# Order of VectorE and ScalarE in the attention stage: pieces, rows, weights and read-outs cut into single-engine steps

## The chip, the cores and the metric

The kernel runs on one core of one Trainium2 chip. The metric is device time in microseconds (us) of one execution; the median of several runs counts. TensorE (PE) multiplies matrices and transposes, VectorE (DVE), ScalarE (ACT) and GpSimd (POOL) work on elements, SyncE's queue (SP) issues the transfers (DMAs). Each engine takes its instructions from a queue of its own, in the order in which they stand there, and waits where an operand isn't ready.

## The reference, cut to what matters

One layer of an encoder on x of 2048 tokens by 1024 columns, all in float32:

```python
h = rmsnorm(x, attn_norm_w)
q_a, k_a, v_a, q_b, k_b, v_b, g_b, g_c, x_c = split(h @ w_in)     # 4 heads, 8 heads, 256 channels
y_sb = stick_breaking_attention(q_a, k_a, v_a)                    # sigmoid(z) * prod(1 - sigmoid(z)) over nearer keys
y_ch = chunked_relpos_attention(rms(q_b), rms(k_b), v_b, rel_bias)  # softmax over a band of 576 keys
y_cv = g_b * causal_conv3(g_c * x_c)
x = x + group_rmsnorm(concat(y_sb, y_ch, y_cv)) @ w_out
x = x + swiglu(rmsnorm(x, ffn_norm_w), w_gate, w_up, w_down)      # d_ff = 2816
```

The kernel holds the tokens in reversed order.

## The kernel before

**Stages.** The tokens are worked on in two halves of two groups (512 tokens, four blocks of 128 each). The attention stage (`weave`) holds all projections from w_in, both attentions and the convolution for both halves, and the output projection of the first half. Then come, without a hand-written order, the feed-forward part of the first half (`ffn(0)`), the output projection of the second half and `ffn(1)`.

**Products.** Each float32 product is made of three float16 products with a high and a low part of each factor (`mm3`, L318 to L323). So every weight block is prepared: `load` fetches it (L181) and ScalarE sums its squares (L183), `split` forms a power of two from the sums through one small matmul into a bank `tp` (L206 or L208) and small VectorE instructions (L212 to L220), then ScalarE scales (L225) and rounds it to the high part (L226), GpSimd takes the difference as the low part (L227), and both are stored in DRAM (`wd`, L231) for the next half. `get` hands out one block, splits the next and loads the one after.

**Rows.** Rows of 128 tokens are fetched into tiles `xt` (six buffers, also for `yt` and `xf`), normed by `rms_rows` (a Square on ScalarE, L310, a chain of ten [128,1] instructions, L312 and L103 to L116, and one product, L314, on VectorE), and turned by `to_T` (TensorE L275 into a bank `sc`, ScalarE `hh` L277, VectorE `hl` L278). `Rows.ahead` does a pair of rows; `beside` deals its yields out between the matmuls of a projection, one for every four steps, and `need` runs it at once.

**Pieces.** A stick-breaking piece is up to four key blocks for one block of queries: scores (L608, L611) into a bank `sc`, two sigmoids on ScalarE (`be` L634, `re` L635), on VectorE a running product (L636) and a product (L638). A piece of the chunked attention has up to five blocks: VectorE adds the bias and takes the maximum (L670, L674), ScalarE the exponential (L676), VectorE the factor `f` (L679, L680). Then in both `transposed`: TensorE turns up to four blocks into a bank `tp` (L574; two banks for five blocks), ScalarE reads the bank as `wth` (L576), VectorE as `wtl` (L577). At last `weighted` multiplies with V into the bank `av`, and `put_y` reads it (ScalarE `yu` L599, GpSimd L600, a store on SP L601). PSUM has 2 banks `acc`, 3 `sc`, 2 `tp` and 1 `av`. `piece` and `chunk_tile` hand out three functions: `front`, `mid` (the transposes with their read-outs) and `back`.

**Order.** `weave` walks through the 112 pieces of the first half and the 176 of the second. `fill` is a generator of the projections, which yields an estimate of TensorE's time; `run` advances it up to a clock value, and `later` puts a function off to a clock value. `stage` traces for piece i the `mid` of piece i - 3, then the `back` of piece i - 5, then the `front` of piece i, each followed by a third of the projections that belong to this piece. Only TensorE's queue keeps this order (`manual_schedule` with `engines={PE}`); the queues of the other engines are ordered by the compiler, which estimates when each instruction can start. A read-out (`use`) follows the last matmul of its bank at once.

Of the kernel before, what the change touches and what calls it, by code (L numbers as in the profile page):

```python
# [9 lines left out]
F32 = mybir.dt.float32  # L10
# [30 lines left out]
def trunk(ctx: ExitStack, tc: tile.TileContext, x, anw, w_in, qnw, knw, biasx, conv_w, onw, w_out,  # L41
# [44 lines left out]

    def acc():
        return ps.tile([128, 512], F32, name="acc", tag="acc", bufs=2)

    def sc1():  # L90
        return ps.tile([128, 512], F32, name="sc", tag="sc", bufs=3)

    def tpb():
        return ps.tile([128, 512], F32, name="tp", tag="tp", bufs=2)
# [66 lines left out]
    class Weights:  # L161
# [3 lines left out]
        def __init__(self, plan):  # L165
            self.plan = plan
            self.raw, self.ready = {}, {}
            self.at = 0

        def load(self, n):  # L170
            if n >= len(self.plan) or n in self.raw or self.plan[n] in wd:
                return
            key = self.plan[n]
            shape, one, gain, srcs = block(key)
            ss = small(2, "ws", BF16)
            tiles = []
            for i, unit in enumerate(srcs):
# [4 lines left out]
                with nc.allow_low_precision(reason="a bound, to a factor of two"):  # L182
                    nc.scalar.activation(junk(), raw, AF.Square, accum_out=ss[:, i:i + 1])  # L183
                tiles.append(raw)
            self.raw[n] = ss, tiles

        def split(self, n):
            if n >= len(self.plan) or n in self.ready:
                return
            key = self.plan[n]  # L190
            shape, one, gain, srcs = block(key)
# [9 lines left out]
            ss, tiles = self.raw.pop(n)  # L201
            m = len(tiles)
            o = tpb()
# [5 lines left out]
            c = 1 if one else m  # L209
# [20 lines left out]
            for w, t in zip(made, wd[key]):  # L230
                nc.sync.dma_start(t, w)  # L231
            self.ready[n] = made

        def ahead(self):
            self.split(self.at)
            self.load(self.at + 1)
# [809 lines left out]
```

## Time and profile before

| what | value |
|---|---|
| median of 3 runs | 2725.04 us (2721.22 to 2729.78) |
| the profiled execution | 2726.58 us |
| its span, first to last instruction | 2724.7 us |
| mean granted clock of TensorE | 0.98 of full speed |
| busy: PE, DVE, ACT, POOL | 2539.0, 1467.3, 1079.9, 401.3 us |
| first stage (to about 1180 us): busy PE, DVE, ACT | 1026.4, 914.7, 754.1 us |

An engine's busy time is that in which it executes an instruction; the rest of the span it waits or has nothing to do. Busy time in the two stages differs, so it is read by stretches. The profiled execution's time beyond its span lies around the first and last instruction.

### The profile page before, as it was taken

The page shows a single profiled execution, that of the slowest core. Times are in us where ns is not written, and L with a number is a line of the kernel's source. Part 1 is how long each engine was busy: PE and PEld are TensorE (multiplying, and loading weights), DVE is VectorE, ACT ScalarE, POOL GpSimd, SP SyncE. Part 2 cuts the span into 40 slices and gives each one's busy share as a digit, 9 for nine tenths or more (in the row PEclk, how much of TensorE's full clock was granted, in tenths as well). Part 3 has the DMA queues.
Part 4 walks back from the last instruction along what each step waited for, and adds up shares of the span by engine and source line. Part 5 has one row for each costly group of instructions (what it writes and reads, how often), then busy time and mean ns, then how long its engine had stood idle before and what let it go on. Part 6 is the DMA issues. An engine that isn't in the chain of part 4 may idle for free.

```text
span 2724.7 us, 41834 instructions
## 1 busy us (share of the span) xinstructions
PE 2539.0 (93%) x16258; PEld 1690.5 (62%) x16258; DVE 1467.3 (54%) x3455; ACT 1079.9 (40%) x1994; POOL 401.3 (15%) x469
## 2 busy tenths in 40 slices
PE   5988888998799888979999999999999999999999
PEld 4567766766687577845555555556865555555556
DVE  6467877789989877844443334334342333223233
ACT  5566756666466777762333333320121111111110
POOL 2124331112313121121111121110000000000000
PEclk8999999999899999989999999999999999999999
DMA  7443435434221256372222223222651111111101
GB/s 246 142 128 97 124 112 159 129 123 146 92 81 47 97 167 194 94 271 102 93 93 93 93 99 110 93 101 98 226 194 39 47 47 49 68 47 47 47 24 62
DMA packets 245352, 294.34 MB, mean 108 GB/s; under 512 B 77472, under 2 KB 194208, under 8 KB 245152
## 3 DMA queue, kind: packets, MB, share of 16 engines
q1 hardware_dynamic: 245152, 291.65, 33.2%
q8 instruction: 128, 2.10, 0.3%
q14 instruction: 72, 0.59, 0.1%
HBM read 199.30 MB, written 92.27 MB: 107 GB/s over the span
## 4 chain that ended last, share of the span: by engine, by line
PE 37%; DMA 5%; issue 4%; DVE 2%; POOL 1%; ACT 1%; SPq 1%; POOLq 0%; DVEq 0%; ACTq 0%
PE acc L321 7%; PE acc L322 7%; PE acc L320 7%; PE sc L963 5%; PE sc L965 5%; PE sc L964 5%; DMA x1d<-xs 2%; DMA wr<-in_w_down 1%; POOL w L227 1%; DMA wr<-in_w_up 1%; PE sc L275 0%; DVE gl L949 0%; DVE wl L260 0%; DVE x L967 0%; ACT wh L258 0%
## 5 line engine op out<-in xcount | busy, mean ns | idle before, releaser
L321 PE MATMUL acc<-hl,w 128*128 128x512 f16 x1728 | 656.1, 380 | 0.2 <-DVE hl L278 0.2
L320 PE MATMUL acc<-hh,w 128*128 128x512 f16 x1728 | 656.2, 380 | 0.0
L322 PE MATMUL acc<-hh,w 128*128 128x512 f16 x1728 | 655.9, 380 | 0.0
L945 DVE SCALAR_TENSOR_TENSOR sg<-acc,ds,sg 128x512 f32<-128x512 f32 x88 | 66.0, 750 | 614.8 <-PE acc L322 539.5
L320 PE MATMUL acc<-w,hh 128*128 128x256 f16 x1408 | 391.6, 278 | 4.0 <-ACT w L226 4.0
L321 PE MATMUL acc<-w,hh 128*128 128x256 f16 x1408 | 391.6, 278 | 1.8 <-POOL w L227 1.8
L322 PE MATMUL acc<-w,hl 128*128 128x256 f16 x1408 | 391.3, 278 | 0.0
L967 DVE TENSOR_TENSOR x<-sc,x 128x512 f32<-128x512 f32 x352 | 241.4, 691 | 211.0 <-PE sc L965 203.6
L322 PEld LDWEIGHTS <-w 128*128 128x128 f16 x1728 | 169.3, 98 | 205.3 <-issue 2.2
L963 PE MATMUL sc<-wh,gh 128*128 128x512 f32 x704 | 282.3, 401 | 4.6 <-DVE x L967 4.5
L320 PEld LDWEIGHTS <-w 128*128 128x128 f16 x1728 | 169.4, 98 | 183.9 <-issue 5.6
L321 PEld LDWEIGHTS <-w 128*128 128x128 f16 x1728 | 169.3, 98 | 180.1 <-issue 0.6
L965 PE MATMUL sc<-wh,gl 128*128 128x512 f32 x704 | 278.0, 395 | 0.0
L964 PE MATMUL sc<-wl,gh 128*128 128x512 f32 x704 | 277.9, 395 | 0.0
L227 POOL TENSOR_TENSOR w<-wr,w 128x1024 f16<-128x1024 f32 x76 | 162.4, 2157 | 547.1 <-ACT w L226 463.9
L577 DVE SCALAR_TENSOR_TENSOR wtl<-tp,wth 128x512 f16<-128x512 f32 (+3 forms) x384 | 200.2, 530 | 46.9 <-ACT wth L576 45.9
L636 DVE TENSOR_TENSOR_SCAN re<-re,zero 128x512 f32<-128x512 f32 (+3 forms) x160 | 187.7, 1173 | 63.2 <-ACT re L635 63.0
L576 ACT ACTIVATE wth<-tp 128x512 f16<-128x512 f32 (+3 forms) x384 | 176.1, 475 | 81.2 <-PE tp L574 80.2
L948 ACT CAST gh<-sg 128x512 fp32r<-128x512 f32 x88 | 54.3, 617 | 384.4 <-DVE sg L945 384.4
L225 ACT ACTIVATE wr<-wr,wsc 128x1024 f32<-128x1024 f32 x76 | 83.4, 1142 | 194.5 <-DVE wsc L216 194.2
L321 PEld LDWEIGHTS <-hh 128*128 128x128 f16 x1408 | 140.5, 100 | 31.5 <-issue 5.7
L963 PEld LDWEIGHTS sc<-wh,gh 128*128 128x128 f32 x704 | 132.5, 188 | 41.3 <-DVE x L967 8.9
(167 smaller groups left out, 3776.2 us busy)
## 6 DMA issues: line engine op xcount, KB each, us to landing
w<-wd SPq DMA_DIRECT2D x92, 512.0 KB, 4.1
wd<-w SPq DMA_DIRECT2D x76, 512.0 KB, 2.7
wr<-in_w_down SPq DMA_DIRECT2D x44, 512.0 KB, 4.4
q<-qd SPq DMA_DIRECT2D x192, 64.0 KB, 2.3
wr<-in_w_gate SPq DMA_DIRECT2D x22, 512.0 KB, 4.4
wr<-in_w_up SPq DMA_DIRECT2D x22, 512.0 KB, 5.4
xt<-in_x SPq DMA_DIRECT2D x16, 512.0 KB, 4.7
wr<-in_w_in SPq DMA_DIRECT2D x16, 512.0 KB, 5.3
```

Source lines behind the costliest of these rows:

```text
L225: nc.scalar.activation(raw, raw, AF.Copy, scale=sc[:, 0:1] if one else sc[:, i:i + 1])
L227: nc.gpsimd.tensor_tensor(w[:, 1, :], raw, w[:, 0, :], ALU.subtract)
L320: nc.tensor.matmul(o, sh(k), mh(k), start=(k == 0), stop=False)
L321: nc.tensor.matmul(o, sh(k), ml(k), start=False, stop=False)
L322: nc.tensor.matmul(o, sl(k), mh(k), start=False, stop=(k == n - 1))
L576: nc.scalar.activation(wh[:, s], tp[:, c], AF.Copy, scale=WSC)
L577: nc.vector.scalar_tensor_tensor(wl[:, s], tp[:, c], WSC, wh[:, s], op0=ALU.mult, op1=ALU.subtract)
L636: nc.vector.tensor_tensor_scan(re, re, zero.to_broadcast([128, N]), 1.0 if b == T else e[:, 0:1], ALU.mult, ALU.add)
L963: nc.tensor.matmul(o, gh[:, cs], wh[:, cc], start=st, stop=False)
L964: nc.tensor.matmul(o, gh[:, cs], wl[:, cc], start=False, stop=False)
L965: nc.tensor.matmul(o, gl[:, cs], wh[:, cc], start=False, stop=en)
L967: nc.vector.tensor_tensor(x1, o, x1, ALU.add)
```

## The change

VectorE and ScalarE join TensorE: their queues keep the order in which the program is traced in the first stage. For that the program is cut into steps that hold the work of one engine where that was done:

- A piece is one generator (`steps`). A `beat` is a third of a `stage`; on each beat every piece in flight counts down and, at zero, is advanced by one step; a yield gives the number of beats to the next. TensorE's scores, then a beat later the next engine's step, and so on. Of the two sigmoids, `re` is now the first.
- PSUM banks carry a note (`Bank`) of whether their read-out has been traced. Who asks for a bank whose last holder's hasn't been has it traced then.
- Read-outs of projections are traced 0.8 us of the projections' clock later (`behind`), those of `to_T` after its yield.
- A weight block's Squares move from `load` to `split`; `split` is a generator, which `start` begins 2.0 us after a `get` and goes on with after 3.0 us and 1.5 us for each tile.
- Rows are fetched a pair ahead, and `rms_rows` norms a pair with [128,2] instructions (13 in the chain), in a step for ScalarE and one for VectorE, whose yields are 0.0. `y_norm`'s rows are fetched 5 us before their norm.
- After the first stage these steps are run through at once (`stream.paced = False`).

Repeated adaptions to the new return values are left out.

```diff
+        def read(self, what):
+
+            def once():
+                if not self.done:
+                    self.done = True
+                    what()
+            self.force = once
+            return once
+
...
+    def bank(name, bufs, cols=512):
+        ring = Bank.rings.setdefault(name, [])
+        if len(ring) == bufs:
+            old = ring.pop(0)
+            while not old.done:
+                old.force() if old.force is not None else advance(old.piece)
+        ring.append(Bank())
+        return ps.tile([128, cols], F32, name=name, tag=name, bufs=bufs), ring[-1]
...
-            for i, unit in enumerate(srcs):
+            for unit in srcs:
                 raw = wp.tile([128, D], F32, name="wr", tag="wr", bufs=4)
                 rv = raw.rearrange(f"p ({shape[0]}) -> p {shape[0]}", **shape[1])
                 for put, src in unit:
                     nc.sync.dma_start(put(rv), src)
-                with nc.allow_low_precision(reason="a bound, to a factor of two"):
-                    nc.scalar.activation(junk(), raw, AF.Square, accum_out=ss[:, i:i + 1])
                 tiles.append(raw)
-            self.raw[n] = ss, tiles
+            self.raw[n] = tiles
...
             self.load(n)
-            ss, tiles = self.raw.pop(n)
+            shape, one, gain, srcs = block(key)
+            tiles = self.raw.pop(n)
+            self.ready[n] = made = []
             m = len(tiles)
-            o = tpb()
+            c = 1 if one else m
+            ss = small(2, "ws", BF16)
+            for i, raw in enumerate(tiles):
+                with nc.allow_low_precision(reason="a bound, to a factor of two"):
+                    nc.scalar.activation(junk(), raw, AF.Square, accum_out=ss[:, i:i + 1])
+            yield 3.0
+            o, bk = tpb()
...
-            made = []
+            wd[key] = [dp.tile([128, 2, D], F16, name=f"wd{len(wd)}_{i}") for i in range(m)]
             for i, raw in enumerate(tiles):
+                yield 1.5
                 w = wp.tile([128, 2, D], F16, name="w16", tag="w16")
                 nc.scalar.activation(raw, raw, AF.Copy, scale=sc[:, 0:1] if one else sc[:, i:i + 1])
                 nc.scalar.copy(w[:, 0, :], raw)
                 nc.gpsimd.tensor_tensor(w[:, 1, :], raw, w[:, 0, :], ALU.subtract)
+                nc.sync.dma_start(wd[key][i], w)
                 made.append(w)
-            wd[key] = [dp.tile([128, 2, D], F16, name=f"wd{len(wd)}_{i}") for i in range(m)]
...
+        def start(self, n, after=0.0):
+            self.steps[n] = self.split(n)
+            if self.paced:
+                later(after, lambda: self.more(n))
+            else:
+                run_all(self.steps[n])
+
+        def more(self, n):
+            after = next(self.steps[n], None)
+            if after is not None:
...
-            self.split(n)
+            if n not in self.steps:
+                self.steps[n] = self.split(n)
+            run_all(self.steps[n])
             self.load(n + 1)
-            if n:
-                self.ahead()
-            else:
-                later(6.0, self.ahead)
+            self.start(n + 1, 2.0)
+            self.load(n + 2)
...
         for i in range(2):
-            p = sc1()
+            p, bk = sc1()
             ks = slice(4 * i, 4 * i + 4)
             for k in range(4):
                 c = (4 * i + k) * 128
                 nc.tensor.transpose(p[:, k * 128:(k + 1) * 128], xn[:, c:c + 128], ident)
-            pk = p.rearrange("p (k c) -> p k c", k=4)
-            nc.scalar.copy(hh[:, ks, cs], pk)
-            nc.vector.tensor_tensor(hl[:, ks, cs], pk, hh[:, ks, cs], ALU.subtract)
+
+            def parts(pk=p.rearrange("p (k c) -> p k c", k=4), ks=ks):
+                nc.scalar.copy(hh[:, ks, cs], pk)
+                nc.vector.tensor_tensor(hl[:, ks, cs], pk, hh[:, ks, cs], ALU.subtract)
+
+            parts = bk.read(parts)
             yield 0.45
+            parts()
...
+    def rms_rows(tiles, gain):
+
+        a = small(2, "sa")
+        for i, xt in enumerate(tiles):
+            nc.scalar.activation(junk(), xt, AF.Square, accum_out=a[:, i:i + 1])
+        yield 0.0
+        nc.vector.tensor_scalar(a, a, -0.5 / D, -0.5 * EPS, op0=ALU.mult, op1=ALU.add)
+        r = rsqrt(a, 2, "rr")
+        for i, xt in enumerate(tiles):
+            nc.vector.scalar_tensor_tensor(xt, xt, r[:, i:i + 1], gain, op0=ALU.mult, op1=ALU.mult)
+        yield 0.0
...
+                tiles = self.get(g, t)
+                if t == 0:
+                    self.get(g, 2)
+                if self.norm is not None:
+                    yield from self.norm(tiles)
+                for b, xt in zip((t, t + 1), tiles):
+                    yield from to_T(xt, *self.H[g], b)
+                del self.got[g, t]
...
+    def behind(what):
+        if stream.paced:
+            later(0.8, what)
+        else:
+            what()
...
-            use(g, o)
+            behind(bk.read(lambda g=g, o=o: use(g, o)))
...
+        parts = [(0, 3), (3, 5)] if n == 5 else [(0, n)]
+        tps = []
+        for b0, b1 in parts:
+            tps.append(tpb())
+            for b in range(b0, b1):
+                nc.tensor.transpose(tps[-1][0][:, (b - b0) * 128:(b - b0 + 1) * 128],
+                                    src[:, b * 128:(b + 1) * 128], ident)
+        yield
+        for (tp, bk), (b0, b1) in zip(tps, parts):
+            nc.scalar.activation(wh[:, b0 * 128:b1 * 128], tp[:, :(b1 - b0) * 128], AF.Copy, scale=WSC)
+        yield
+        for (tp, bk), (b0, b1) in zip(tps, parts):
+            bk.done = True
             s = slice(b0 * 128, b1 * 128)
-            c = slice(0, (b1 - b0) * 128)
-            for b in range(b0, b1):
-                nc.tensor.transpose(tp[:, (b - b0) * 128:(b - b0 + 1) * 128],
-                                    src[:, b * 128:(b + 1) * 128], ident)
-            nc.scalar.activation(wh[:, s], tp[:, c], AF.Copy, scale=WSC)
-            nc.vector.scalar_tensor_tensor(wl[:, s], tp[:, c], WSC, wh[:, s], op0=ALU.mult,
+            nc.vector.scalar_tensor_tensor(wl[:, s], tp[:, :(b1 - b0) * 128], WSC, wh[:, s], op0=ALU.mult,
...
     def put_y(T, head, av, f):
+        av, bk = av
+        yield
+        bk.done = True
         u = ap.tile([128, 2 * HD], F32, name="yu", tag="yu")
         nc.scalar.activation(u, av, AF.Copy, scale=f)
+        yield
         nc.gpsimd.tensor_tensor(u[:, :HD], u[:, :HD], u[:, HD:], ALU.add)
...
+            def steps():
+                z, bk = scores(Q, cols, K, (b - k0) * 128, N, b == T)
+                yield
+                bk.done = True
...
+                nc.scalar.activation(re, z, AF.Sigmoid, scale=ZS[head // 2][:, 1:2])
                 nc.scalar.activation(be[:, :N], z, AF.Sigmoid, scale=ZS[head // 2][:, 0:1])
-                nc.scalar.activation(re, z, AF.Sigmoid, scale=ZS[head // 2][:, 1:2])
+                yield
                 nc.vector.tensor_tensor_scan(re, re, zero.to_broadcast([128, N]),
                                              1.0 if b == T else e[:, 0:1], ALU.mult, ALU.add)
                 MUL.tensor_tensor(be[:, 0:N], be[:, 0:N], e[:, 0:N], ALU.mult)
-
-            def mid():
-                r["T"] = transposed(r["w"], n)
-
-            def back():
+                yield 5
+                w = yield from turned(be, n)
+                yield 5
                 if b == T:
                     state["av"] = open_av()
                 av = state["av"]
-                weighted(av, *r["T"], [V[:, b + i - k0] for i in range(n)], b == T, b + n == NB)
+                weighted(av[0], *w, [V[:, b + i - k0] for i in range(n)], b == T, b + n == NB)
                 if b + n == NB:
...
-            for i, (a, w) in enumerate(parts):
-                z = scores(Q, cols, K, c0 + a, w)
+            zs = [scores(Q, cols, K, c0 + a, w) for a, w in parts]
+            yield
+            for i, ((z, bk), (a, w)) in enumerate(zip(zs, parts)):
+                bk.done = True
...
+            yield
...
+            yield 2
             f = small(1, "f")
             nc.vector.reciprocal(f, tot)
             nc.vector.tensor_tensor(f, f, VS[head], ALU.mult)
-            r["s"], r["f"] = s, f
...
+            yield 3
+            w = yield from turned(s, n)
+            yield 5
             av = open_av()
...
-                later(6.0 * (4 * i + t), lambda T=g * 4 + t: y_norm(
-                    T, gain, lambda: ap.tile([128, 520], F32, name="ysq", tag="w2")))
+                def start(T=g * 4 + t):
+                    yt = y_fetch(T)
+                    later(5.0, lambda: y_norm(T, yt, gain, lambda: ap.tile([128, 520], F32, name="ysq", tag="w2")))
+
+                later(6.0 * (4 * i + t), start)
...
+        def beat(gap):
+
+            for p in list(line):
+                p[0] -= 1
+                if p[0] == 0:
+                    advance(p)
+            run(clock[0] + gap / 3)
+
+        def stage(p, half, gap):
+            beat(gap)
+            beat(gap)
+            line.append([1, p, half])
+            beat(gap)
+
...
+                    spent += BLK * p[1]
+                    stage(p[0], half, max(0.0, origin + at * step - spent - clock[0]))
+        while line:
+            beat(1.0)
         run(1e9)
+        stream.paced = False
...
-        with tc.manual_schedule(engines={mybir.EngineType.PE}):
+        with tc.manual_schedule(engines={mybir.EngineType.PE, mybir.EngineType.DVE, mybir.EngineType.Activation}):
```

## Rows read from the trace of the kernel before

**Rows 1.** The page's busy line, and the span in 40 slices, in tenths.
```profile
PE 2539.0 (93%) x16258; PEld 1690.5 (62%) x16258; DVE 1467.3 (54%) x3455; ACT 1079.9 (40%) x1994; POOL 401.3 (15%) x469
...
PE   5988888998799888979999999999999999999999
...
DVE  6467877789989877844443334334342333223233
```

**Rows 2.** Stretches: busy PE, PEld, DVE, ACT, POOL; granted clock, DMA share, GB/s.
```profile
0.00:60.00 60.00, 26.24 (x192) 22.67 (x193) 40.68 (x140) 35.65 (x57) 14.18 (x21) 0.86 0.76 249
60.00:320.00 260.00, 237.88 (x1924) 174.21 (x1922) 163.98 (x343) 162.83 (x305) 76.22 (x100) 0.97 0.42 130
320.00:360.00 40.00, 28.67 (x248) 23.54 (x249) 37.65 (x149) 26.04 (x56) 18.05 (x20) 0.83 0.29 89
360.00:580.00 220.00, 205.00 (x1683) 143.56 (x1681) 156.92 (x530) 137.18 (x321) 45.15 (x89) 0.99 0.50 146
580.00:760.00 180.00, 151.47 (x1338) 116.39 (x1337) 175.13 (x347) 103.58 (x193) 49.36 (x49) 0.96 0.33 105
760.00:1180.00 420.00, 377.18 (x3626) 306.46 (x3625) 340.35 (x961) 288.80 (x604) 93.97 (x143) 0.98 0.39 117
1180.00:1220.00 40.00, 26.72 (x117) 14.68 (x116) 22.15 (x65) 26.29 (x39) 9.02 (x4) 0.79 0.89 313
1220.00:2725.00 1505.00, 1485.80 (x7142) 889.02 (x7140) 530.41 (x925) 299.54 (x422) 95.39 (x44) 1.00 0.25 86
```

**Rows 3.** TensorE's waits, 60 to 1180 us: total, times, longest.
```profile
PE tp L574 <- DVE wtl L577: 41.0, 36, 4.2
...
PE tp L517 <- DVE wtl L577: 10.6, 7, 2.7
...
PE tp L517 <- DVE qrt L111: 6.5, 1, 6.5
```

**Rows 4.** Timeline at 228 to 236 us: ScalarE, TensorE.
```profile
228.18 2.19 ACT L225 ACTIVATE wr<-wr,wsc 128x1024 f32<-128x1024 f32 x2
230.26 1.99 ACT L226 CAST w<-wr 128x1024 f16<-128x1024 f32 x2
...
235.39 1.11 PE L574 MATMUL tp<-ident,be 128*128 128x128 f32 x4 [4.21 <-DVE wtl L577]
```

**Rows 5.** Timeline at 1052 to 1059 us: ScalarE, VectorE, TensorE.
```profile
1055.75 1.06 ACT L310 ACTIVATE junk<-xf 128x1024 bf16<-128x1024 f32 x1 [3.75 <-DMA xf<-x1d]
...
1056.93 0.15 DVE L312 TENSOR_SCALAR sa<-ss 128x1 f32<-128x1 f32 x1 [4.03 <-ACT junk L310]
...
1059.04 1.02 PE L574 MATMUL tp<-ident,s 128*128 128x128 f32 x5 [4.65 <-DVE f L679]
```

**Rows 6.** Groups by line and shape, 60 to 1180 us: busy, mean ns, idle before.
```profile
L496 POOL TENSOR_TENSOR qs<-qk 128x512 f32<-128x512 f32 x32 | 37.3, 1166 | 46.2 <-ACT qk L494 46.2
...
L183 ACT ACTIVATE junk<-wr 128x1024 bf16<-128x1024 f32 x28 | 29.8, 1064 | 23.0 <-DMA wr<-in_w_in 22.9
L500 DVE TENSOR_REDUCE qa<-qs 128x8 f32<-128x512 f32 x32 | 21.7, 677 | 11.7 <-POOL qs L496 9.6 <-POOL re L630 1.9
...
L314 DVE SCALAR_TENSOR_TENSOR xf<-xf,rry,gain 128x1024 f32<-128x1024 f32 x4 | 5.1, 1281 | 0.0
```

**Rows 7.** Timeline of the start: TensorE's wait, ScalarE ahead of it.
```profile
36.81 1.05 ACT L310 ACTIVATE junk<-xt 128x1024 bf16<-128x1024 f32 x1
...
45.55 1.94 PE L275 MATMUL sc<-ident,xt 128*128 128x128 f32 x8 [15.56 <-DVE xt L314]
```

**Rows 8.** Timeline of VectorE: a solid chain, then a woven one.
```profile
233.78 0.18 DVE L111 TENSOR_TENSOR qrt<-qrt,qa 128x16 f32<-128x16 f32 x1
233.99 0.17 DVE L113 SCALAR_TENSOR_TENSOR qry<-qrt,qry 128x16 f32<-128x16 f32 x1
...
694.84 0.17 DVE L111 TENSOR_TENSOR qrt<-qrt,qa 128x16 f32<-128x16 f32 x1
694.93 0.68 DVE L740 TENSOR_REDUCE ya<-ysq 128x8 f32<-128x512 f32 x1
```

More of the change, by code (lines that the diff above doesn't have):

```diff
@@ L85, in trunk, with __init__, advance @@
     ynd = [dp.tile([128, D], F32, name=f"ynd{t}") for t in range(NB)]
+    class Bank:
+        rings = {}
+        def __init__(self):
+            self.done = False
+            self.piece = running[0]
+            self.force = None
+        def read(self, what):
[5 more added lines that the diff above has]
+            return once
+    running = [None]
+    def bank(name, bufs, cols=512):
[6 more added lines that the diff above has]
+        return ps.tile([128, cols], F32, name=name, tag=name, bufs=bufs), ring[-1]
     def acc():
-        return ps.tile([128, 512], F32, name="acc", tag="acc", bufs=2)
+        return bank("acc", 2)
     def sc1():
-        return ps.tile([128, 512], F32, name="sc", tag="sc", bufs=3)
+        return bank("sc", 3)
     def tpb():
-        return ps.tile([128, 512], F32, name="tp", tag="tp", bufs=2)
+        return bank("tp", 2)
+    def advance(p):
+        before, running[0] = running[0], p
+        wait = next(p[1], "over")
+        running[0] = before
+        if wait == "over":
+            line.remove(p)
+            traced[p[2]] -= 1
+        else:
+            p[0] = wait or 1
+    line = []
+    traced = [None, None]
     def small(n, name, dt=F32):
@@ L227, in split @@
                 nc.gpsimd.tensor_tensor(w[:, 1, :], raw, w[:, 0, :], ALU.subtract)
+                nc.sync.dma_start(wd[key][i], w)
                 made.append(w)
-            wd[key] = [dp.tile([128, 2, D], F16, name=f"wd{len(wd)}_{i}") for i in range(m)]
[L230 to L236, printed above, removed]
+        def start(self, n, after=0.0):
[7 more added lines that the diff above has]
+            if after is not None:
+                later(after, lambda: self.more(n))
         def get(self, key):
@@ L391, in beside, with normed, norm, fetch @@
             yield from more
+    def normed(key):
+        gain = []
+        def norm(tiles):
+            if not gain:
+                gain.append(gain_row(key))
+            yield from rms_rows(tiles, gain[0])
+        return norm
     def x_rows(H, groups):
-        gain = []
-        def make(g, b):
+        def fetch(g, b):
             xt = xp.tile([128, D], F32, name="xt", tag="xt")
@@ L399, in make, with fetch @@
             nc.sync.dma_start(xt, x[r0:r0 + 128, :])
-            if not gain:
-                gain.append(gain_row("a"))
-            return rms_rows(xt, gain[0])
-        return Rows(H, groups, make)
+            return xt
+        return Rows(H, groups, fetch, normed("a"))
     def y_rows(H, groups):
-        def make(g, b):
+        def fetch(g, b):
             yt = xp.tile([128, D], F32, name="yt", tag="xt")
@@ L748, in y_norms @@
     def y_norms(half):
[L749 removed]
+        assert traced[half] == 0, (half, traced)
         groups = HALVES[half]
@@ L777, in ffn_rows, with fetch @@
     def ffn_rows(H, groups):
-        gain = []
-        def make(g, b):
+        def fetch(g, b):
             xt = xp.tile([128, D], F32, name="xf", tag="xt")
             last_row[where(g)[0]] = nc.sync.dma_start(xt, x1d[g * 4 + b])
-            if not gain:
-                gain.append(gain_row("f"))
-            return rms_rows(xt, gain[0])
-        return Rows(H, groups, make)
+            return xt
+        return Rows(H, groups, fetch, normed("f"))
     HF = [{}, {}]
@@ L871, in weave @@
         ends = [whole + start + 8.0, 2 * whole + 11.6 * unit / 1.4]
[L872 to L873 removed]
         BLK = 0.5
[L876 to L887 removed]
+        def beat(gap):
[9 more added lines that the diff above has]
+            beat(gap)
         for half, groups in enumerate(HALVES):
             pieces, blocks = count(half)
+            traced[half] = pieces
             origin = None
```

114 lines of the change are left out of this document (40 added, 74 removed).

## Prediction

> **What bounds the kernel now.** Read the page's first two parts before anything else [rows 1]. TensorE is busy 93% of the span, VectorE 54%, ScalarE 40%; but the slices fall into two stages. In the first 17 (1,160 us, the attention stage) VectorE stands mostly at 6 to 9 tenths and TensorE between 5 and 9; behind them, but for the slice of the change-over, TensorE is at 9. So the second stage is TensorE's, and whatever an order of VectorE and ScalarE is worth must come out of the first. The table of stretches gives the amount [rows 2]. TensorE stands idle 60 - 26.2 = 33.8 us up to 60 us, 22.1 us from 60 to 320, 11.3 from 320 to 360, 15.0 from 360 to 580, 28.5 from 580 to 760 and 42.8 from 760 to 1180: 119.7 us after the start. From 1220 on it is 19 us in 1,505.
>
> In two of these stretches VectorE is itself full: 37.65 of 40 us, and 175.13 of 180. Those hold 39.8 us of the idle time, and no order alone makes VectorE's work there smaller. In the other three it is at 63%, 71% and 81%, and TensorE still waits: 79.9 us. The granted clock adds to it: (1 - clock) times the stretch is 7.8, 2.2 and 8.4 us there, 18.4 together, time lost at the lower of the two levels, 1.2 GHz, around stalls.
>
> What TensorE waits for is in the list of waits [rows 3]: first of all transposes into a bank `tp` that VectorE has not read yet, 41.0 us at L574 and 10.6 at L517. VectorE was late, though not full. Two places show why. At 228 us ScalarE begins four instructions of one weight block, 4.1 us in a row, while the copy `wth` stands behind them; when TensorE goes on at 235.39 it has stood 4.21 us for the `wtl` that needs it [rows 4]. At 1052 us ScalarE stands 3.75 us in front of a Square whose row has not landed; VectorE then waits 4.03 us for that Square with other work behind it, and TensorE 4.65 [rows 5]. Both are an engine held, in its own order, by work that could have waited.
>
> **The change part by part.** The sum is made against the profiled execution: 2726.58 us, 1.9 us over its span and 1.5 over the median of 2725.04.
>
> *TensorE's order of the attention pieces stays.* Before, transposes come in the first third of the third stage after the scores: 7 thirds; products with V 14. Afterwards 1+1+5 and again 1+1+5 beats: the same. A beat is 1,120 us over 3 x 288 pieces (112 in the first half of the tokens, 176 in the second, by `count`), 1.3 us. What changes is when the other two engines' steps stand in their own queues, one beat after the step that feeds them. Price on TensorE itself: 0.
>
> *Weight blocks.* The Squares leave `load` and are queued one `get` later, when the block's transfer is long done; ScalarE's wait for these transfers is 22.9 us in this stage [rows 6]. The two tiles of a block are copied 1.5 us of projection time apart, so what stands in a row is half of 2.19 + 1.99, 2.1 us. The DMAs are the same in number; a store `wd` is issued per tile, earlier if anything, behind `yu`'s stores on SP as before.
>
> *Rows.* Fetches go ahead by a pair, so the stall at 1052 us has no successor from the second pair on; the first pair of each series is still fetched where it is normed. Sixteen x rows in eight pairs take 13 small VectorE instructions a pair instead of 20: about 7 x 0.1 us, 3 us for the four pairs at 320 to 360 where VectorE is full.
>
> *What these and the beats give back.* Of 79.9 + 18.4 = 98.3 us in the stretches where VectorE is not full, bounds are 0 (every late `wtl` is replaced by another) and 98. I take one half, 49 us: the two patterns shown are those that the change takes apart, but the named instances are a part of 36 waits at L574 alone, and a strict order makes new ones (below). Where VectorE is full I take 0.
>
> *Start.* TensorE's longest wait of all, 15.56 us to 45.55, has its cause in ScalarE's queue: the Square that the transposes need begins only at 36.81, behind a whole weight block, and three Squares of later rows stand ahead of the rest [rows 7]. Afterwards a pair's two Squares stand together, behind the block's Squares and ahead of its copies: 4.2 us for the copies [rows 4] and 3 x 1.06 for the Squares [rows 5], 7 of the 15.6 us, come back. Against it three more x tiles are fetched ahead of the gain and the first weights: 128 x 1024 x 4 bytes each at the 249 GB/s of this stretch [rows 2] is 2.1 us, 6.3 at most, and 0 if another wait ends last; I take 3. Net -4; bounds -12 and +6.
>
> *Chains of small instructions.* Each `rsqrt` becomes one block on VectorE: 13 instructions of which each needs the one before. The trace shows such instructions 0.21 us apart when nothing stands between, and 0.09 us each when big ones do [rows 8]. So a chain that is woven in now and solid afterwards costs 13 x 0.12 = 1.6 us more. From 580 to 760 there are 8 of `y_norm` and 3 or 4 of the query norms: 18 us if all are woven in now, 0 if none. The trace there shows both kinds; I take +10, in full, since VectorE is the bound there. The Trainium skill speaks otherwise ("VectorE: DVE Perf Modes", The DRAIN you can't avoid): eight copies took 13.88 us with a semaphore after each and without, so a dependent chain costs nothing extra. By that the term would be 0 and the sum 10 us lower. The row of this trace, 0.21 against 0.09 us on these short ones, says otherwise and decides here.
>
> *Norm steps directly ahead of their transposes.* The yields of `rms_rows` are 0.0. In `beside` each still buys four projection steps; in `between` and in `out_proj` nothing lies between, and TensorE's transposes stand behind 2 x 1.06 us on ScalarE, then 13 x 0.21 + 2 x 1.28 = 5.3 us on VectorE: up to 7.4 us [rows 5, 6, 8]. Behind the waiting transposes stand projections and the pieces' own steps. Such are one x pair and two f pairs, 22 us; for the three pairs in `beside` 5.3 less 2.5 us (1.3 of projection, about as much attention), 8 more. The other bound is 0: both engines may run ahead of TensorE. I take 15.
>
> *Read-outs.* They are queued 0.8 us late; `chunk_qk` still puts ScalarE's copy, GpSimd's square (1.17 us) and VectorE's reduce in one step, 32 times [rows 6]. VectorE now stands through GpSimd's 1.17 us with the next `wtl` behind; 9.6 us of that stand in the list already. It costs nothing while VectorE runs behind ScalarE by a beat, and up to 32 x 1.2 = 37 us where it does not. I leave it inside the half not recovered above.
>
> *Second stage.* No manual order, the same matmuls. ScalarE is at 20% there: 299.5 of 1,505 us [rows 2]. The Squares move by one `get`, some 20 us earlier than needed either way. 0, bounds -5 and +5 (the idle 13.3 us at 1180 to 1220 may move).
>
> Sum: -49 - 3 - 4 + 10 + 15 = -31: 2695.6 as profiled, 2694 for the median.
>
> **The rivals.**
>
> *A: solid blocks take the place of the woven ones; slower.* In program order `y_norm` is 2 x 0.68 + 13 x 0.21 and a product like L314's 1.28, 5.4 us on VectorE (8 times), a pair of rows 5.3 us (6 after the start), a query norm 0.68 + 2.7 = 3.4 us (16), and no `wtl` can pass. A stick piece has four beats, 5.2 us, from `wtl` to the transposes that need its bank; a chunk piece of five blocks uses both banks and has one, 1.3 us. If half of them meet the short one, 4 x 4.1 + 3 x 4.0 + 8 x 2.1 = 45 us; with half of the reduce's 37 us and the 25 for chains and transposes that is 88, against 49 + 3 + 4 recovered: +32, 2757. For it: VectorE is at 78% over the stage (874 of 1,120 us, the sum of the five stretches), so a 5 us block takes some 20 us to work off. Against: such work is on the same engine now, and TensorE already stands behind it (6.5 us at L111 [rows 3]). It decides where blocks and reduces cost more than 56 - 25 = 31 us.
>
> *B: no change.* VectorE's work (874 us of 1,120) and the pace of the pieces, which is computed as before, set the stage's length; idle time moves to other places. What is gained in the open stretches is waited for in the full one. -8 to +8: 2725.
>
> *C: much more.* If nearly all waits on late read-outs go and the clock's loss with them, 80 of 98 us return and the transposes never stand behind the norms: -80 - 3 - 4 + 10 = -77: 2648.
>
> **How the numbers follow.** 0.3% is 8 us, about what a measurement tells from no change. The forecast (-8 to -60 us) has 0.47, C 0.12, B 0.14, A 0.27. Faster is 0.59, same 0.14, slower 0.27. The likeliest case's own range is 2665 to 2717; the range for 8 in 10 reaches over B into A, and to the edge of C: 2645 to 2755.
>
> **What would show it.** Right: first stage ends 25 to 35 us earlier, at about 1130; waits of `tp` on `wtl` below half of their 52 us; no ScalarE Square waiting for `wr`; the longest wait of the start near 9 us; 580 to 760 as long as before or longer, with VectorE at 97%. Wrong, towards A: waits of transposes on the norm (L314's successor) above 20 us, VectorE's waits for GpSimd above 25 us, VectorE below 78% while TensorE's idle time grows. Wrong, towards B: idle time falls in the open stretches and rises in the full one by as much. The second stage, 1,505 us, should stay within 5 us; if it doesn't, the prediction has missed a part.

## The result and the profile after

The changed kernel takes 2837.50 us (median, 2836.72 to 2846.00); the kernel before took 2723.28 beside it. The ratio is 1.0422 [1.0395, 1.0449]: 114 us slower, and outside the range. The profiled execution took 2836.72, its span is 2834.9.

The page's busy line and slices, to set beside [rows 1]:

```profile
PE 2561.9 (90%) x16258; PEld 1704.5 (60%) x16258; DVE 1499.2 (53%) x3343; ACT 1082.4 (38%) x1994; POOL 401.5 (14%) x469
...
PE   4998877898678887877999999999999999999999
...
DVE  5487667779987787774443333333433322333223
```

TensorE stands at 9 for good from the 20th slice on, 1347 us; before it was the 19th, 1226 us. The stretches, cut where the work is about that of [rows 2]:

```profile
0.00:80.00 80.00, 42.57 (x282) 33.71 (x283) 40.48 (x116) 36.48 (x57) 14.17 (x21) 0.91 0.65 213
80.00:320.00 240.00, 220.97 (x1816) 162.18 (x1815) 165.34 (x329) 158.47 (x295) 74.09 (x97) 0.99 0.41 125
320.00:420.00 100.00, 73.69 (x607) 58.34 (x607) 58.23 (x208) 48.78 (x109) 35.54 (x44) 0.85 0.33 98
420.00:640.00 220.00, 189.63 (x1459) 126.82 (x1458) 157.59 (x464) 127.33 (x293) 31.68 (x70) 0.96 0.43 129
640.00:860.00 220.00, 170.56 (x1438) 134.03 (x1437) 195.42 (x364) 106.14 (x199) 51.85 (x52) 0.89 0.30 94
860.00:1300.00 440.00, 362.08 (x3388) 286.48 (x3387) 338.03 (x914) 275.84 (x580) 84.76 (x135) 0.95 0.34 99
1300.00:1340.00 40.00, 25.75 (x118) 14.51 (x117) 20.42 (x55) 28.12 (x40) 13.22 (x7) 0.83 0.92 323
1340.00:2834.00 1494.00, 1476.62 (x7159) 888.45 (x7157) 523.66 (x897) 301.25 (x425) 96.21 (x45) 1.00 0.26 88
```

The first stage ends at about 1300 us, not 1180. TensorE's idle time between the start and that end, the length less the busy time of five rows, is 19.0 + 26.3 + 30.4 + 49.4 + 77.9 = 203 us; before it was 119.7. Its busy time is 23 us more for as many matmuls (2561.9 against 2539.0), at lower granted clocks: 0.85 from 320 to 420, 0.89 from 640 to 860. VectorE is busy 915 us of these 1,220, 75%, and still what TensorE waits for. The second stage is 10 us shorter.

TensorE's waits from 80 to 1300 us (total, times, longest), to set beside [rows 3]:

```profile
PE tp L660 <- DVE wtl L669: 88.8, 49, 6.5
PE tp L600 <- DVE wtl L669: 26.3, 15, 3.8
PE sc L329 <- DVE xf L373: 16.7, 2, 9.3
PE av L679 <- ACT yu L694: 16.0, 12, 3.1
PE sc L329 <- DVE xt L373: 12.7, 3, 6.2
```

VectorE's waits in the same stretch:

```profile
DVE f L777 <- ACT yu L694: 68.0, 70, 3.9
DVE st L531 <- ACT st L530: 61.8, 31, 4.1
DVE qa L583 <- POOL qs L579: 36.6, 21, 3.1
```

The waits for a late `wtl` have more than doubled, from 41.0 + 10.6 to 88.8 + 26.3 us. And VectorE now stands 166 us in three places: 68.0 us before the factor `f`, whose buffer ScalarE has not read yet, 61.8 before the read-out `st` behind ScalarE's, and 36.6 before the reduce `qa` behind GpSimd's square. The longest of TensorE's waits for `wtl` shows how they hang together; this is the timeline at 326 to 337 us, VectorE, ScalarE, GpSimd and TensorE:

```profile
326.69 0.75 ACT L664 ACTIVATE wth<-tp 128x384 f16<-128x384 f32 x2
...
326.82 0.17 DVE L777 RECIPROCAL f<-tot 128x1 f32<-128x1 f32 x1 [2.67 <-ACT yu L694]
327.02 1.72 DVE L778 TENSOR_TENSOR f<-f,vs 128x1 f32<-128x1 f32 x1
...
326.60 2.13 POOL L276 TENSOR_TENSOR w<-wr,w 128x1024 f16<-128x1024 f32 x1 [4.11 <-ACT w L275]
...
331.57 1.04 POOL L579 TENSOR_TENSOR qs<-qk 128x512 f32<-128x512 f32 x1 [2.56 <-ACT qk L577]
...
332.64 0.69 DVE L583 TENSOR_REDUCE qa<-qs 128x8 f32<-128x512 f32 x1 [2.77 <-POOL qs L579]
333.36 0.17 DVE L587 TENSOR_SCALAR qa<-qa 128x16 f32<-128x16 f32 x1
...
335.87 0.17 DVE L159 TENSOR_TENSOR qry<-qry,qrt 128x16 f32<-128x16 f32 x1
335.96 0.88 DVE L669 SCALAR_TENSOR_TENSOR wtl<-tp,wth 128x384 f16<-128x384 f32 x2
...
336.56 1.33 PE L660 MATMUL tp<-ident,s 128*128 128x128 f32 x5 [6.49 <-DVE wtl L669]
```

The `wth` that `wtl` needs is done at 327.44. In program order stand ahead of `wtl`: `f`, whose buffer of four pieces ago is still to be read by ScalarE's `yu` (2.67 us); the reduce `qa` behind GpSimd's square (2.77 us); and behind that 13 small instructions 0.21 us apart. `wtl` begins 8.5 us late, TensorE stands 6.49.

### The profile page after: what moved, and what is told of

Same layout as the page of the kernel before. It is cut to its first block, busy times and chain, and to the rows that moved or that the text cites. A ratio compares the mean times of both kernels' runs of the same rounds, so it can differ in the third digit from the quotient of the medians.

```text
span 2834.9 us, 41790 instructions
## 1 busy us (share of the span) xinstructions
PE 2561.9 (90%) x16258; PEld 1704.5 (60%) x16258; DVE 1499.2 (53%) x3343; ACT 1082.4 (38%) x1994; POOL 401.5 (14%) x469
## 5 line engine op out<-in xcount | busy, mean ns | idle before, releaser
L733 DVE TENSOR_TENSOR_SCAN re<-re,zero 128x512 f32<-128x512 f32 (+3 forms) x160 | 200.4, 1252 | 22.3 <-ACT re L730 22.1
L679 PE MATMUL av<-v,wth 128*128 128x128 f16 x1104 | 146.3, 226 | 16.0 <-ACT yu L694 16.0
```

The costliest lines, as they stand in the source:

```text
L679: nc.tensor.matmul(av, wh[:, i * 128:(i + 1) * 128], vs[i], start=first and i == 0, stop=last and i == n - 1 > 0)
L733: nc.vector.tensor_tensor_scan(re, re, zero.to_broadcast([128, N]), 1.0 if b == T else e[:, 0:1], ALU.mult, ALU.add)
```

## The experiments

A change of less than 8 us is not told from none. Each ratio is to runs of the kernel before on the same chip. "After" is the changed kernel.

**Which engine's order.** The recut kept, and the set of engines that hold to the program's order cut down:

```diff
-with tc.manual_schedule(engines={mybir.EngineType.PE, mybir.EngineType.DVE, mybir.EngineType.Activation}):
+with tc.manual_schedule(engines={mybir.EngineType.PE}):     # e1; with DVE: e2; with Activation: e3
```

TensorE's own order is that of after in e3, and in e1 and e2 but for one small matmul of a weight block near the stage's end.

> The changed program with one word less: only TensorE's queue keeps the program's order, VectorE and ScalarE are ordered by the compiler again; all steps stay cut as in the change. Theory 1 (the fixed order holds what stands behind a late step): the loss of 114 us goes, 2680 to 2735 us. Theory 2 (the cut itself costs it: read-outs 0.8 us late, weight copies apart, rows normed in pairs): it stays at 2810 to 2845.

> TensorE and VectorE keep the program's order, ScalarE is ordered by the compiler. Theory 1a (VectorE's fixed order is the holder, with 68 us of waits at the reciprocal of f, 62 at st and 37 at qa): 2800 to 2840 us. Theory 1b (ScalarE's order is): 2700 to 2750. If both are needed, between.

> TensorE and ScalarE keep the program's order, VectorE is ordered by the compiler. Theory 1a (VectorE's fixed order holds): 2700 to 2750 us. Theory 1b (ScalarE's): 2800 to 2840.

Measured: e1 2690.41, 0.9879 [0.9862, 0.9897]; e2 2794.17, 1.0263 [1.0248, 1.0279]; e3 2710.93, 0.9958 [0.9941, 0.9974]. So the recut alone is 33 us faster than before, VectorE's fixed order costs 104 on top of that, ScalarE's 20 alone and 43 on top of VectorE's. e1 and e3 came as theory 1 and 1a say; e2 lies 6 us under 1a's interval, as ScalarE's order has a share too. In e1's timeline of VectorE a chain of the query norm is woven again, with a `wtl` and an `st` inside:

```profile
225.43 0.17 DVE L156 SCALAR_TENSOR_TENSOR qry<-qrt,qry 128x16 f32<-128x16 f32 x1
225.51 0.68 DVE L669 SCALAR_TENSOR_TENSOR wtl<-tp,wth 128x512 f16<-128x512 f32 x1
226.11 0.17 DVE L153 TENSOR_TENSOR qrt<-qry 128x16 f32<-128x16 f32 x1
...
226.61 0.74 DVE L531 SCALAR_TENSOR_TENSOR st<-tp,nw,st 128x512 f16<-128x512 f32 x1
```

What the recut gave is not fewer late `wtl`: TensorE's waits of the first 1200 us in e1 are

```profile
PE tp L660 <- DVE wtl L669: 54.8, 38, 4.6
PE sc L329 <- DVE xt L373: 17.3, 3, 14.7
...
PE tp L600 <- DVE wtl L669: 12.0, 8, 2.9
...
PE tp L660 <- DVE qry L147: 4.1, 1, 4.1
...
PE tp L660 <- DVE be L735: 3.4, 2, 1.9
```

66.8 us for `wtl`, against 51.6 in [rows 3]. What fell are the waits for `xt`, 27.9 us in before, those behind a chain, 6.5 us in [rows 3] and 4.1 here, and those of transposes behind other work of VectorE, which in before are

```profile
PE tp L574 <- DVE be L638: 10.4, 6, 3.4
PE tp L574 <- DVE f L679: 8.6, 4, 4.7
```

**The named places, with all three orders fixed.** `f` in 8 buffers (e4); with it the read-outs of the query and convolution transposes split between ScalarE and VectorE, and the reduce queued 2 us behind GpSimd's square (e8b); the chains of the query norm and of `y_norm`, and `y_norm`'s product, in parts (e10); the row norms a pair ahead (e7); all of it (e12); the row norms in parts too (e17). e8b, e7 and the two runs built on them also move some of TensorE's instructions to other places of its queue:

```diff
-f = small(1, "f")                                    # 4 buffers
+f = sp.tile([128, 1], F32, tag="f", bufs=8)          # e4, e8b, e12, e17
...
-put_parts(tp, ...)                                   # ScalarE's st, VectorE's st in one step
+later(0.8, put_high); later(1.6, put_parts)          # e8b, e12, e17
-nc.vector.reduce_sum(a, sq)
+later(2.0, lambda: norms(...))                       # the reduce and what follows
...
-r = rsqrt(a, 16, "qr")                               # and "yr"
+r = yield from rsqrt_steps(a, 16, "qr")              # a part each 0.5 us: e10, e12, e17
...
+later(2.0, self.prepare)                             # norm of the next pair: e7, e12, e17
```

> The changed kernel with eight buffers in place of four for the factor f of the chunked attention, nothing else. VectorE's reciprocal then no longer waits for the ScalarE read-out of the piece four before, which is queued one beat ahead of it, behind weight copies. Theory A (this buffer is what holds VectorE in the chunked pieces, 68 us of waits): 2770 to 2805 us. Theory B (it is covered by the other late steps): 2820 to 2840.

> The changed kernel with three held places mended, and the same fixed order of all three engines: f in 8 buffers; the read-outs of the query transposes and of the convolution split into ScalarE's step and VectorE's step 0.8 us of projection time apart; the reduce of the query squares queued 2.0 us behind GpSimd's square. Theory H (late operands hold VectorE's queue: in the trace after it stands 68.0 us in f behind yu, 61.8 in st behind ScalarE's st, 36.6 in qa behind GpSimd): more than half of the 104 us that VectorE's order cost goes, 2750 to 2785. Theory S (solid blocks of small chains hold the queue, H's waits are cover): 2815 to 2835.

> The changed kernel with the solid blocks broken up: the reciprocal-root chains of the query norms and of y_norm, and y_norm's product, are queued in parts 0.5 us of projection time apart, so that other steps of VectorE stand between them; nothing else is changed. Theory S (rival A of the prediction: blocks of 3.4 and 5.4 us that no wtl can pass): 24 chains x 2 to 4 us go, 2765 to 2795. Theory H (late operands): 2825 to 2845, since each part still stands behind the same waits.

> The changed kernel with the row norms of the first stage queued one pair ahead of the transposes that need them, not directly ahead; nothing else is changed. Theory N (the prediction's term for norms directly ahead of their transposes, 15 us taken, 30 at most): TensorE's waits for xt and xf, 29.4 us past the start in the trace after, go by half or more: 2808 to 2823. Theories H and S: the wait moves elsewhere, 2828 to 2842.

> All of it together: f in 8 buffers, split read-outs, the reduce deferred, row norms a pair ahead, chains spread, and still the fixed order of all three engines. If the named places H, S and N are the whole loss, the time comes to what the recut gave with TensorE's order alone plus what the ScalarE order cost there: 2700 to 2730. If the loss is that an engine held to program order cannot pass ANY late step, wherever it is, the sum of the three mends gives half of it or less: 2765 to 2815.

> As the five mends together (2776 us), and the row norms' small chain and two products on VectorE are queued in parts 0.5 us of projection time apart as well. In that run's trace one such block, 436.18 to 441.27 us with 1.35 us of waiting for ScalarE ahead of it, holds a wtl, and TensorE stands 4.54 us for it. If unbroken blocks are what is left of the loss (eleven more pairs of rows, 3 to 5 us each): 2730 to 2755. If what is left is the sum of many small waits for an order that no longer fits the times, of no one place: 2765 to 2790.

Measured: e4 2829.16, 1.0387 [1.0369, 1.0404]; e8b 2783.69, 1.0230 [1.0208, 1.0252]; e10 2802.54, 1.0299 [1.0274, 1.0323]; e7 2840.37, 1.0435 [1.0413, 1.0458]; e12 2775.86, 1.0200 [1.0177, 1.0223]; e17 2766.08, 1.0167 [1.0150, 1.0185]. Against after, the late operands are worth 54 us (e8b) and the solid blocks 35 (e10). Together they give only 62 (e12), with the row norms' blocks 71 (e17). So the two overlap. The timeline above shows it for one `wtl`: late operands and a block hold it one after the other, and when one goes the other is left.

Theory H's interval of 2750 to 2785 holds for e8b. Theory S named a place that counts, but e10 stays above its 2795. Theory N fell: in e7 the waits for `xt` and `xf` are gone from the head of the list, and those of the pieces' transposes for `wtl` have risen from 88.8 to 101.0. e12 and e17 lie where the expectations put a loss of no one place. One that was left in e12 is a row norm, still in one block (VectorE, then TensorE):

```profile
436.18 0.17 DVE L383 TENSOR_SCALAR sa<-sa 128x2 f32<-128x2 f32 x1 [1.35 <-ACT junk L381]
...
438.87 2.48 DVE L386 SCALAR_TENSOR_TENSOR xt<-xt,rry,gain 128x1024 f32<-128x1024 f32 x2
441.27 0.28 DVE L719 SCALAR_TENSOR_TENSOR wtl<-tp,wth 128x128 f16<-128x128 f32 x1
...
441.61 1.11 PE L684 MATMUL tp<-ident,t 128*128 128x128 f32 x4 [4.54 <-DVE wtl L719]
```

**The six mends with fewer orders fixed, and one part of the recut undone.** e19 is e17 with TensorE's order alone, e20 with TensorE's and VectorE's. e18 is e1 with the weight blocks as before: Squares in the load, copies in one step, and the whole `split` at once behind the `get`:

```diff
+nc.scalar.activation(junk(), raw, AF.Square, accum_out=ss[:, i:i + 1])   # in load
-yield 3.0                                                                 # in split
-    yield 1.5
-later(after, lambda: self.more(n))                                        # in start
+run_all(self.steps[n])
```

> The same six mends, with only TensorE's order fixed. If the mends cure nothing but the strict order's own waits, they give nothing where VectorE and ScalarE may pass a late step: 2682 to 2700. If they take away waits that any order meets (the reduce behind GpSimd, f's buffers, norms directly ahead of their transposes): 2655 to 2680.

> The same six mends, with the orders of TensorE and VectorE fixed and ScalarE's free. Without the mends ScalarE's order cost 20 us on top of TensorE's alone and 43 on top of TensorE's and VectorE's. If ScalarE's share of what is left is as before: 2715 to 2740. If VectorE's order alone holds the rest: within 10 us of the run with all three orders fixed.

> The recut with only TensorE's order fixed (2690 us, 33 us under the kernel before), with one part of the recut undone: the weight blocks' Squares stand in the load again and a block's copies are queued in one step, as in the kernel before. If the prediction's first pattern (ScalarE held by a weight block or by a Square whose weights have not landed) gave most of the gain: 2707 to 2722. If the gain came from the row pairs, the fetches ahead and the finer piece steps: 2686 to 2700.

Measured: e19 2710.06, 0.9958 [0.9942, 0.9974]; e20 2758.74, 1.0131 [1.0111, 1.0152]; e18 2709.55, 0.9959 [0.9943, 0.9975]. Where the engines may pass a late step the mends give nothing: e19 lies above both of its intervals, 20 us over e1, of which the placement below explains 7 to 9. With the mends VectorE's order still costs 49 us (e20 less e19), and ScalarE's 7 (e17 less e20).

e18 loses 19 us to e1, so the weight blocks carry that much of the recut. Not by the waits that the prediction named, though: ScalarE's Squares still wait for `wr`, 33.5 us in e1 and 25.1 in e18, and TensorE waits for `wtl` no longer in e18 than in e1 (43.1 and 7.5 us). Which part of that edit counts was not tried.

**What is left of VectorE's 49 us.** e21 spaces `y_norm`'s blocks 14 us apart, not 6; e22 queues the row norms' parts sooner and closer; e23 does both; e24 is e1 with the spacing:

```diff
-later(6.0 * (4 * i + t), start)
+later(14.0 * (4 * i + t), start)      # e21, e23, e24
-later(2.0, self.prepare)              # parts 0.5 us apart
+later(0.3, self.prepare)              # parts 0.25 us apart: e22, e23
```

> The six mends with the orders of TensorE and VectorE fixed (2759 us), and y_norm's blocks queued 14 us apart, not 6: the same work, over more of the first stage. If the rest of the loss is that y_norm's steps, which nobody waits for, stand ahead of wtl where VectorE is nearly full: 15 to 30 us of the 43.3 us there go, 2729 to 2744. If the loss is spread over all waits: 2752 to 2766, as the waits move with the work.

> The six mends with the orders of TensorE and VectorE fixed (2759 us), and the row norms queued 0.3 us behind the pair before (not 2.0) in parts 0.25 us apart (not 0.5), so that they are done when their transposes come. If the transposes' 16.8 us behind the row norm are part of the loss: 2742 to 2752. If they are cover: 2754 to 2764.

> Both at once. If the two places are the rest of the loss: 2712 to 2732. If it is spread: 2750 to 2764.

> The recut with TensorE's order alone fixed (2690 us), and y_norm's blocks 14 us apart. If the spacing cures only what a fixed order makes of it: 2685 to 2695. If VectorE is the bound there under any order (97% busy from 600 to 700 us): 2665 to 2685.

Measured: e21 2760.07, 1.0143 [1.0124, 1.0162]; e22 2756.94, 1.0130 [1.0111, 1.0147]; e23 2755.68, 1.0130 [1.0115, 1.0145]; e24 2687.94, 0.9880 [0.9861, 0.9898]. No change in any, against e20 or e1. But the edits hardly reached the waits that they aimed at (TensorE's waits, 80 to 1300 us, e20 and then e23):

```profile
PE tp L720 <- DVE wtl L729: 83.7, 63, 5.7
PE sc L342 <- DVE xf L392: 21.1, 4, 7.9
PE sc L342 <- DVE xt L392: 16.8, 4, 5.1
```

```profile
PE tp L720 <- DVE wtl L729: 76.5, 62, 5.5
PE sc L342 <- DVE xf L392: 20.0, 4, 8.2
PE sc L342 <- DVE xt L392: 17.2, 4, 5.1
```

So these runs do not clear the two places. Part of the 49 us can be found in the traces. TensorE's order is the same in e19 and e20. They are level at the 1,801st matmul into a bank `acc` (430.9 and 430.2 us); at the 2,001st e20 is 15.0 us behind (487.4 and 502.4). In that stretch TensorE stands 14.7 us for `xt`, which it does not in e19. In e22 and e23 it is 14.7 as well: the row norms still stand there in one block, directly ahead of their transposes (VectorE, then TensorE, e20):

```profile
445.14 0.16 DVE L383 TENSOR_SCALAR sa<-sa 128x2 f32<-128x2 f32 x1
...
447.77 2.48 DVE L392 SCALAR_TENSOR_TENSOR xt<-xt,rry,gain 128x1024 f32<-128x1024 f32 x2
...
449.11 0.91 PE L342 MATMUL sc<-ident,xt 128*128 128x128 f32 x4 [4.51 <-DVE xt L392]
```

In e12, with the norms a pair ahead, TensorE doesn't wait for `xt` there, but the stretch takes as long (73.7 us; e20 72.2, e19 56.5): the waits are now for `wtl`, 9.9 us, one of them at 441.61 above, and for other steps of VectorE. So some 15 of the 49 us lie in this stretch of three row norms, and moving the norms only moved the waits. Whether norms really cut into parts would give them back was not tried, and what makes up the rest, later in the stage, stays open.

**The second stage.** TensorE does the same work there in the same order, but for two instructions, and yet at two rates: before has 1,810 matmul records in 400 us in which TensorE is full, after 1,824; e4 and all runs with `f` in 8 buffers have 1,809 or 1,810. In the compiled programs `gh` and `gl` begin 128 bytes per partition lower in after (the small tile `ss`, 4 buffers, is gone), and the 8 buffers put them back. One unused tile moves them too. It moves every tile placed behind it, but of what TensorE reads in this stage `gh` and `gl` alone:

```diff
+sp.tile([128, 96], F32, tag="pad")    # b_pad: the kernel before, 384 bytes
+sp.tile([128, 32], F32, tag="pad")    # e26: e1, 128 bytes
```

> The kernel before, with one tile of 384 bytes per partition in the pool of small tiles, so that the second stage's gh and gl begin 384 bytes further on, at the same distance from a multiple of 512 bytes as in the changed kernel. Theory P (the place of these tiles sets the pace of the second stage's matmuls): 1,824 records in 400 us, 2707 to 2713. Theory R (the recut gave all of the 33 us): 1,810 records, 2717 to 2725.

> The recut with TensorE's order alone fixed (2690 us), with one tile of 128 bytes per partition in the pool of small tiles, so that gh and gl stand where they stand in the kernel before. Theory P: 1,810 records in 400 us, 2699 to 2706. Theory R: 1,824 records, 2686 to 2694.

Measured: b_pad 2709.24, 0.9952 [0.9938, 0.9965]; e26 2697.44, 0.9911 [0.9899, 0.9924]. b_pad is as theory P says; e26 lies between the intervals of P and R, with the records of P. The 400 us that begin 600 us ahead of the end, as stretches, in before, b_pad and e26:

```profile
2124.00:2524.00 400.00, 400.00 (x1810) 228.33 (x1808) 117.32 (x160) 46.78 (x65) 0.00 (x0) 1.00 0.15 52
```

```profile
2112.00:2512.00 400.00, 400.00 (x1824) 231.26 (x1823) 119.52 (x164) 45.77 (x64) 0.00 (x0) 1.00 0.15 52
```

```profile
2098.00:2498.00 400.00, 400.00 (x1810) 228.31 (x1808) 116.17 (x159) 46.13 (x64) 0.00 (x0) 1.00 0.14 51
```

The matmuls of this stretch that read `gh` and `gl`, by line, in before and then in b_pad:

```profile
L963 PE MATMUL sc<-wh,gh 128*128 128x512 f32 x192 | 76.9, 400 | 0.0
L965 PE MATMUL sc<-wh,gl 128*128 128x512 f32 x192 | 75.8, 395 | 0.0
```

```profile
L963 PE MATMUL sc<-wh,gh 128*128 128x512 f32 x199 | 78.6, 395 | 0.0
L965 PE MATMUL sc<-wh,gl 128*128 128x512 f32 x199 | 77.5, 389 | 0.0
```

The place alone gives before 12.6 us, and takes 7 to 9 from e1. So e1's 33 us are some 20 to 24 of recut and 9 to 13 of placement, and the mends with `f` in 8 buffers are worth as much more in the first stage than their times say.

This also shows what the recut's gain hangs on. e18 runs its second stage at the faster rate (1,824 records), as b_pad does, and its 0.9959 is no better than b_pad's 0.9952. The first stage says the same: in the profiled executions the first `gh` is written at 1190.6 us in before, 1166.5 in e1 and 1191.7 in e18. With the weight blocks as before, the row pairs, the fetches ahead and the finer steps give nothing by themselves.

## Why the prediction was wrong, point by point

**The step that failed** is the term of 49 us, and in it the bounds "0 (every late `wtl` is replaced by another) and 98". Zero is not a bound: an order can make more late `wtl` than there were. What a strict order makes new was left inside the half not recovered, so it could never cost more than it gave. Measured, the recut gave about 22 us in the first stage, VectorE's order took 104 and ScalarE's, on top of it, 43. The 22 hang on the weight blocks, the first of the two patterns that the term named (e18), but did not come by the waits that it counted: those for `wtl` are 66.8 us in e1 and 50.6 in e18, against 51.6.

**Rival A had the direction**, but not the size or the whole cause: its 88 us of cost stand against 147 measured, its 56 of gains against about 22, and its 2757 against 2837. Its solid blocks are worth 35 us (e10), the late operands, of which it had half of one, 54. Its marks were named and came: VectorE's waits for GpSimd 36.6 us (25), VectorE 75% (78) while TensorE's idle time grew by 83, the transposes' waits for the norm 29.4 past the start (20).

- Read-outs: half of 37 us in A, nothing in the sum. The three late places together are worth 54 (e8b), with the placement's share some 65. So waits counted off as cover ("while VectorE runs behind ScalarE by a beat") were not all covered. The largest of the three, `f` behind `yu` (68.0 us; 19.4 in the trace of before), was in no term. With 8 buffers it goes and gives 8 us (e4), some 17 with the placement's share: most of that one is cover. Whether `st` or `qa` carries the rest was not tried.
- Chains: +10 was taken, 35 is what breaking them up brings alone (e10). The size was 13 x 0.12 on VectorE; what counts is who stands behind. In after the chain runs at 2.68 us for 13 (333.36 to 336.04), 0.21 each, as in [rows 8]. The prediction set against this the Trainium skill ("VectorE: DVE Perf Modes", The DRAIN you can't avoid), whose eight copies take 13.88 us with a semaphore after each and with one after the last alone. That section measures copies, not chains as short as these; here the trace decides again.
- Norms directly ahead of transposes: +15 was taken. Moving them alone changes nothing (e7), since `wtl` is then waited for; with the other mends in place, the stretch of three of them still costs about 15 us (e20 against e19).
- ScalarE's order had no term of its own; it costs 43. In after ScalarE waits 84.1 us for `nm` and 72.2 for the transposes at L600 (44.9 and 25.8 in e1), with other work behind. That these waits make the 43 was not tried.
- Start: net -4 was taken. With TensorE's order alone the waits for `xt` are 17.3 us in e1 (27.9 in the trace of before), but little of that lasts: the 200th matmul into `acc` starts 8.4 us earlier than in before (60.5 and 68.9), the 400th only 2.5 (112.2 and 114.7). With VectorE's and ScalarE's order fixed these waits are 29.4 us, the longest 17.5 against the 15.56 of [rows 7] and the 9 forecast. The order lost it, not the fetches.
- Squares: in after none of the first stage waits for `wr`, as forecast; with ScalarE's order free they still do (33.5 us in e1), and the time is better.
- The first stage ended 120 us later, not 25 to 35 earlier (the "about 1130" beside it does not fit an end at 1180); no stretch kept VectorE at 97%. Second stage: 10 us shorter, outside the 5 allowed. The cause, the place of `gh` and `gl`, was nowhere in the argument.

**What was right:** the sign of what the recut gives by itself. That the sum's 31 us come near the 20 to 24 is luck, as other waits gave them, with VectorE and ScalarE free. That TensorE's own order costs nothing agrees with e1, but was not priced by itself.

The fastest version run is e1, the recut with TensorE's order alone: 2690.41, 0.9879 of before, 147 us under after. e24, with 2687.94, can't be told from it.

## What to carry to other kernels

Cutting work into single-engine steps and holding an engine to their order are two changes: price and run them apart. The first may pay while the second costs many times as much, since in a fixed order each late operand also delays all that is ready behind it. Count, for each fixed engine, the steps that wait for another engine and what stands behind each, and give the cost no upper bound at the waits of today. When a kernel's tiles change, compare a stage that the change does not touch: here an unused tile, which moves the place of others, changed the kernel's time by 0.5%. And when a mend changes nothing, look in its trace whether the wait that it aims at has gone.

## What the runs showed of the hardware that was not expected

- The float32 matmuls of the second stage take 400 and 395 ns (`wh` with `gh`, and the other two products) with `gh` beginning at byte 146,048 of a partition, and 395 and 389 with 145,920 or 146,432. These two are multiples of 512, the other is 128 above one; whether that is the rule was not tried. The addresses are those of the compiled programs.
- The product `f` of 128 x 1 took 1.72 us at 327.02 and ended when GpSimd's product of 2.13 us did (328.74 and 328.73); the reciprocal ahead of it, with one input from SBUF, took 0.17 while the same product ran. The Trainium skill ("GPSIMD Engine Reference", 1. Specifications) says that GpSimd contends with VectorE instructions that have two SBUF inputs; the trace agrees.
